# Copies of key and query rows on GpSimd, turned attention blocks in two buffers, block 0 scored earlier: a two-layer decoder trunk

## The chip, the cores and the metric

The kernel runs on one core of a Trainium2 chip. A core has TensorE (matmuls; PE in the profile, PEld its weight loads), VectorE (DVE), ScalarE (ACT), GpSimd (POOL) and SyncE (SP, which here does nothing but issue DMAs), each with a queue of its own that it works off in order. The metric is the device time of one execution in microseconds (us); less is better.

## The reference

Two layers of a decoder trunk over 528 tokens (16 learned meta tokens and 512 of the sequence), 1024 channels. Each layer:

```
h = RMSNorm(x)
[u_pool | z_pool | c_q | c_kv | k_rope | z_mla | g_pool | g_mla] = h @ W_in
y_pool = W_pool_up( PoolMix(u_pool) * silu(z_pool) )
y_mla  = W_mla_up( MLA(c_q, c_kv, k_rope) * silu(z_mla) )
x = x + W_out( sigmoid(g_pool) * y_pool + sigmoid(g_mla) * y_mla )
```

MLA is causal attention of 8 heads. Queries and keys of a head have 64 plain channels and 32 rotary ones, 96 in all, and are normalized over these 96; the rotary part of the key is shared by the heads up to that factor. Values have 64 channels. Everything is float32.

## The kernel before

**Split products.** Each float32 operand is split into a high and a low part, and a product is three matmuls: high by high, high by low, low by high (`mm3`, lines 202, 203, 204). A weight tile comes by DMA into `raw` (line 133, issued by SP), ScalarE makes `whi` (L197), VectorE subtracts and makes `wlo` (L198). `raw`, `whi` and `wlo` have three buffers each.

**Order of the work.** All projections stand in one list (`plan`), which the generator `stream` turns into matmuls bit by bit; each step tells how many nanoseconds of matmuls it put in, and these add up to a clock of the program, `clk`. The attention is written by hand around it: `gap()` and `fill_now()` put matmuls of the list in until the clock has gone on by so much, and `after(ns, fn)` calls `fn` once the clock has gone on by `ns`. `behind(a, b)` makes `a` wait for `b`; `newest` is the last matmul of the list. A scheduler then sets the final order on each engine, so a line's place in the text isn't its place in the queue.

**A head** (`head`, called by `go` for h = 0 to 7 in each layer). The 512 queries are four blocks of 128. Block i sees the 16 meta tokens and the blocks up to itself, so 144, 272, 400 and 528 keys.
- First half: scores of block 1 and of the first `SPL` = 240 keys of block 3 into one PSUM bank (`sa`), of block 2 into another (`sb`). `top` (L824, VectorE) adds the mask, scales, and takes the extreme of each row; `expo` (L831, ScalarE) takes the exponential and the sum of the row. After a `gap`, `turn` moves the 16 meta columns aside (`pm`, L834, GpSimd) and turns blocks 1 and 2 in 32 by 32 pieces (L837, VectorE) into `attD`, a single buffer of 1280 columns.
- Then `pv` of the head before the last (values by probabilities, L950 and L953), and for an odd head the keys of the next pair (`keys`: L779, then the split).
- Second half, after another `gap`: the other 288 keys of block 3, block 0 (three passes, L872) and, in layer 0, the meta queries (L872), in a third bank. Then `top`, `expo`, and `turn` of blocks 3 and 0.
- Out and back: the reciprocal sums go to DRAM (L894), `attD` goes to the DRAM buffer `pdr` in four DMAs (L899) and comes back in one as `attE` (L901), which swaps the 32-row groups; the sums come back spread over 64 partitions (L902). For an odd head `meta_turn` does the like with the meta columns: one store (L916), three loads (L918); GpSimd multiplies the gate by the sums (L906).
- After two more `gap`s: `parts` (L928, L929) splits `attE` for `pv`.

**Keys and queries of a head** (`prep`, called ahead of the head). A head needs one tile with 64 plain and 32 rotary rows for `kh`, `kl`, `qh` and `ql`. The plain rows of the queries are split in place (L791, L794). The other rows come from tiles where they lie on other partitions, by DMAs from SBUF to SBUF that SP issues: 64 rows of the keys for an even head (L797), 32 rotary rows of the keys (L799) and of the queries (L801). That is six DMAs for an even head and four for an odd one. `keys` of the next pair has two buffers, and an even head's tile is the one that the odd head before it has read.

SP issues all of it: weights (L133), the row copies, the stores and loads of the blocks, of the sums and of the meta columns. A DMA that has to wait holds all that stand behind it.

Of the kernel before, what the change touches and what calls it, by code (L numbers as in the profile page):

```python
# [53 lines left out]
RESERVE = ("gm3", "gm3")  # L54
LAG = 2000.0
TAIL = (9000.0, 9000.0)
SPL = 240
RET = 12500.0
WARM = 8
NB = 10  # L60


# [16 lines left out]
def trunk(ctx, tc, xT, xrow, mrow, pos, win, wkr, wqb, wkb, wvb, wgr, wpu, wmu, wout, gains, const, yT):  # L79
# [20 lines left out]
    def tmp(w=W):  # L100
        return tp.tile([P, w], F32, tag="tmp", name=nm("tmp"), bufs=3)

    def att(tag):
        return sl.tile([P, NB * P], F32 if tag == "D" else F32R, tag=f"att{tag}", name=nm(f"att{tag}"), bufs=1 if tag == "D" else 2)

    def wide():
        return tp.tile([P, NB * P], F32R, tag="th", name=nm("th"), bufs=2)
# [1 line left out]
    def halves():  # L109
        for k in range(4, 8):  # L110
            for a, b in FULL:
                yield xb[:, k, a:b]
        for tag in "DE":
            t = att(tag)
            for a in range(4):
                yield t[:, HALF * a:HALF * a + HALF].bitcast(F32)

    def mmt():
# [222 lines left out]
    class Layer:  # L341
# [441 lines left out]
        def prep(self, h):  # L783
            p, odd = h // 2, h % 2
            n0, r0 = (64, 0) if odd else (0, 64)
            kd = self.ks[p][odd]
            g0 = 32 * (h % 4)
            qh, ql = qhl[odd]
            x0 = self.x0
            src = self.qn[p][n0:n0 + 64, x0:T]  # L790
            made = act.activation(qh[n0:n0 + 64, x0:T], src, AF.Copy)  # L791
            if h == 0:
                behind(made, newest[0])
            dve.tensor_sub(ql[n0:n0 + 64, x0:T], src, qh[n0:n0 + 64, x0:T].bitcast(F32))  # L794
            if odd == 0:
                for d, f in zip(kd, self.ks[p][1]):
                    sp.dma_start(d[0:64, :].bitcast(F32), f[0:64, :].bitcast(F32))  # L797
            for d, f in zip(kd, self.kr[h // 4]):
                sp.dma_start(d[r0:r0 + 32, :].bitcast(F32), f[g0:g0 + 32, :].bitcast(F32))  # L799
            for d, f in zip((qh, ql), self.qr[h // 4]):  # L800
                sp.dma_start(d[r0:r0 + 32, x0:T].bitcast(F32), f[g0:g0 + 32, x0:T].bitcast(F32))  # L801
            m = P if odd else QK
            return [t[0:m] for t in (*kd, qh, ql)]

        def head(self, h, kq, prev):
            kh, kl, qh, ql = kq
            odd = h % 2
            nqs = self.nqs
            pa, pb, pc = slot("pa", w=416), slot("cq8"), slot("cq10")
            bia = sm.tile([P, 5], F32, tag="bia", name=nm("bia"), bufs=2)  # L810
            rs = sm.tile([P, 5], F32, tag="rs", name=nm("rs"), bufs=2)
            if odd == 0:
                self.pm = sm.tile([P, 4, 32], F32, tag="pm", name=nm("pm"), bufs=2)
                self.rb = slot("cq11")
            pm, rb = self.pm, self.rb
            blocks = att("D")
            grid = blocks.rearrange("p (b s r) -> p b s r", b=4, s=NB)

            def scores(i, out, a, b):
                q0 = NM + P * i  # L820
                return mm3(out, qh[:, q0:q0 + P], ql[:, q0:q0 + P], kh[:, a:b], kl[:, a:b], True, True)

            def top(i, c, sv, mask):
                return dve.tensor_tensor_reduce(out=sv, in0=sv, in1=mask, scale=nqs[:, i, h:h + 1], scalar=3e38,  # L824
                                                op0=ALU.add, op1=ALU.min, accum_out=bia[:, c:c + 1])

            def causal(n):
                return maskw[:, 512 - n:]

            def expo(i, c, sv, pv):  # L830
                act.activation(pv, sv, AF.Exp, scale=-1.0, bias=bia[:, i:i + 1], accum_out=rs[:, c:c + 1])  # L831

            def turn(i):
                gp.tensor_copy(pm[:, i, 16 * odd:16 * odd + 16], pt[i][:, 0:NM])  # L834
                for j, n in ((0, i + 1),) if i in (0, 1, 3) else ((0, 2), (2, 1)):
                    k = block(i, j)
                    ins = dve.transpose(grid[:, :, k:k + n, :].rearrange("p b s r -> p s b r"), pt[i][:, NM + P * j:NM + P * (j + n)])  # L837
# [9 lines left out]
            top(3, 4, s3, maskw[:, 0:SPL])  # L847
            sb = sct()
            s2 = sb[:, 0:400]
            scores(2, s2, 0, 400)  # L850
            top(2, 2, s2, causal(400))
            expo(1, 1, s1, pt[1])
            expo(2, 2, s2, pt[2])
            if h == 1:
# [12 lines left out]
            sc = sct()  # L867
            s0, s4 = sc[:, 0:144], sc[:, 144:144 + T - SPL]
            scores(3, s4, SPL, T)

            def passes(out, q0, n):
                return [lambda k=k, q=q, x=x: pe.matmul(out, q[:, q0], x[:, 0:n], start=k == 0, stop=k == 2)  # L872
                        for k, (q, x) in enumerate(((qh, kh), (qh, kl), (ql, kh)))]

            todo = passes(s0, slice(NM, NM + P), 144)
            if not self.last:
                sm_ = sc[0:NM, 432:432 + NM]
                todo += passes(sm_, slice(0, NM), NM)
            for fn in todo:
                fn()  # L880
            if not self.last:
                dve.tensor_add(self.smeta[:, h, :], sm_, cst[0:NM, C_MM:C_MM + NM])
            top(3, 3, s4, causal(T - SPL))
            top(0, 0, s0, causal(144))
# [3 lines left out]
            expo(0, 0, s0, pt[0])  # L888
# [4 lines left out]
            row = rdr[self.l][h]  # L893
            sp.dma_start(row.rearrange("a (p i) -> p (a i)", i=4), rs[:, 0:4])  # L894
            got = att("E")
            n = NB * 32
            via = pdr[h % 2]
            for a in range(4):
                sp.dma_start(via[:, n * a:n * a + n].rearrange("(b k) x -> k b x", k=32),  # L899
                             blocks[32 * a:32 * a + 32, :].rearrange("p (b x) -> p b x", x=n))  # L900
            sp.dma_start(got.bitcast(F32), via)  # L901
            sp.dma_start(rb[64 * odd:64 * odd + 64, 0:512], row.partition_broadcast(64))  # L902
            if odd == 1:
                self.meta_turn(pm)
                z = self.zms[h // 2][:, NM:T].rearrange("p (i q) -> p i q", i=4)
                gp.tensor_mul(z, z, rb[:, 0:512].rearrange("p (q i) -> p i q", i=4))  # L906
            return h, got

        def meta_turn(self, pm):
            t = slot("cq9", F32R)  # L910
            f, hi, lo = t[:, 0:P], t[:, P:2 * P], t[:, 2 * P:3 * P]
            dve.transpose(f.bitcast(F32), pm.rearrange("p i r -> p (i r)"))
            split(hi, lo, f.bitcast(F32), 0, P)
            self.mt = slot("racc", F32R)
            via = mdr[0]
            sp.dma_start(via, t[:, P:3 * P].bitcast(F32))  # L916
            for g, c in ((0, 0), (32, 1), (64, 0)):
                sp.dma_start(self.mt[g:g + 32, 0:512].bitcast(F32).rearrange("p (a x) -> p a x", a=4),  # L918
                             via[:, P * c:P * c + P].rearrange("(a r) x -> r a x", a=4))

        def parts(self, prev):
            if prev is None:
                return None
            h, got = prev
            hi, f = wide(), got.bitcast(F32)
            for a in (0, NB * 64):
                b = a + NB * 64
# [336 lines left out]
```

## Time and profile before

| | |
|---|---|
| runs shown | 777.93, 776.76, 777.90 us, median 777.9 |
| profiled execution | 770.3 us, its span 768.5 |
| mean granted TensorE clock | 0.995 |
| TensorE, VectorE, ScalarE, GpSimd busy | 757.2, 537.7, 393.3, 141.1 us |
| attention of layer 0, of layer 1 | about 175 to 310 us, 564 to 690 us |

The profile comes from one execution. Busy shares say how full an engine was. The timeline lists instructions with their start and length; matmuls are pipelined, so their lengths overlap, and what one costs is the distance to the next start. The brackets behind a line tell how long the engine stood idle before it and what released it. The chain of waits follows the work back from the end: at each step what had to come last. "SPq" there is SP issuing a DMA, "DMA a<-b" a transfer under way.

### The profile page before, as it was taken

To read this page: it belongs to the slowest core of one execution; us is meant where nothing else is said; L and a number is where in the kernel's file an instruction comes from. 1 tells how busy PE (TensorE), PEld (TensorE's weight loads), DVE (VectorE), ACT (ScalarE), POOL (GpSimd) and SP (SyncE) were. 2 spreads that over 40 slices of the span, in tenths; PEclk is the share of its full clock that TensorE was granted. 3 is DMA by queue.
4 is the path that set the end of the run, shared out by engine and by line. 5 is a ranking of instruction groups with operands and counts; after the bars stand their busy time and mean duration, and the time that the engine had idled before them with its cause. 6 is when DMAs were issued, how large, how long until landed. Compare 5 with 4: busy or idle time off the path is not lost.

```text
span 768.5 us, 14306 instructions
## 1 busy us (share of the span) xinstructions
PE 757.2 (99%) x5028; PEld 689.0 (90%) x5028; DVE 537.7 (70%) x1211; ACT 393.3 (51%) x864; POOL 141.1 (18%) x187
## 2 busy tenths in 40 slices
PE   9999999999999899999999999999999999999998
PEld 9999999999989899999997898887788788788887
DVE  4588787358889887684366477774578799776832
ACT  5755655545556555543255445455445556554320
POOL 2026404000101010052130264030001110112400
PEclk9999999999999999999999999999999999999999
DMA  7532323336765667425542323234457677673363
GB/s 261 181 109 84 100 80 104 118 124 165 200 201 164 179 201 204 141 83 147 177 143 93 114 83 100 80 89 132 127 158 197 197 207 206 187 214 105 121 196 108
DMA packets 77204, 113.03 MB, mean 147 GB/s; under 512 B 15382, under 2 KB 36246, under 8 KB 77132
## 3 DMA queue, kind: packets, MB, share of 16 engines
q1 hardware_dynamic: 76988, 111.86, 48.4%
q8 instruction: 39, 0.64, 0.3%
q14 instruction: 33, 0.27, 0.1%
q10 hardware_dynamic: 144, 0.26, 0.1%
HBM read 89.76 MB, written 15.86 MB: 137 GB/s over the span
## 4 chain that ended last, share of the span: by engine, by line
PE 85%; DVE 6%; DMA 5%; SPq 1%; issue 1%; ACT 1%; DVEq 0%; ACTq 0%
PE mm L202 26%; PE mm L204 25%; PE mm L203 25%; DMA raw<-win 2%; PE S L202 2%; PE S L204 2%; PE S L203 2%; DVE wlo L198 1%; DVE S L824 1%; DMA kh<-kh 1%; DMA pdr<-attD 1%; PE S L528 1%; PE o L950 1%; PE o L953 1%; DMA mdr<-cq 1%
## 5 line engine op out<-in xcount | busy, mean ns | idle before, releaser
L202 PE MATMUL mm<-hh,whi 128*128 128x264 f32 (+2 forms) x1072 | 338.9, 318 | 5.9 <-ACT whi L197 4.0
L204 PE MATMUL mm<-hh,wlo 128*128 128x264 f32 (+2 forms) x1072 | 338.4, 318 | 0.2 <-DVE wlo L198 0.2
L203 PE MATMUL mm<-hl,whi 128*128 128x264 f32 (+2 forms) x1072 | 337.9, 316 | 0.0
L198 DVE TENSOR_TENSOR wlo<-raw,whi 128x512 fp32r<-128x512 f32 (+2 forms) x242 | 172.5, 715 | 108.5 <-ACT whi L197 103.3
L197 ACT ACTIVATE whi<-raw 128x512 fp32r<-128x512 f32 (+2 forms) x242 | 144.4, 600 | 181.2 <-PE mm L203 126.8
L202 PEld LDWEIGHTS mm<-hh,whi 128*128 128x128 f32 x1072 | 202.7, 189 | 20.2 <-ACT whi L197 4.9
L203 PEld LDWEIGHTS mm<-hl,whi 128*128 128x128 f32 x1072 | 202.8, 189 | 12.4
L204 PEld LDWEIGHTS mm<-hh,wlo 128*128 128x128 f32 x1072 | 202.2, 189 | 12.7 <-DVE wlo L198 0.6
L834 POOL COPY pm<-cq 128x16 f32<-128x16 f32 x32 | 13.3, 416 | 216.5 <-ACT cq L831 216.5
L824 DVE CUSTOM_DVE_ANT_0 S<-S,maskw,nqs 128x240 f32<-128x240 f32 (+4 forms) x80 | 38.3, 499 | 2.3 <-PE S L204 1.7
L642 POOL TENSOR_TENSOR racc<-racc,tmp 128x264 f32<-128x264 f32 (+1 forms) x15 | 14.3, 957 | 134.8 <-ACT tmp L641 134.8
L1025 POOL TENSOR_TENSOR tmp<-tmp,xb 128x264 f32<-128x264 f32 (+1 forms) x24 | 27.1, 1142 | 55.2 <-DVE tmp L1023 53.3
L831 ACT ACTIVATE cq<-S,bia 128x400 f32<-128x400 f32 (+2 forms) x48 | 24.4, 512 | 25.0 <-DVE bia L824 11.9
L202 PE MATMUL mm<-cq,whi 128*128 128x264 f32 (+1 forms) x108 | 34.8, 322 | 0.0
L203 PE MATMUL mm<-th,whi 128*128 128x264 f32 (+1 forms) x108 | 34.7, 321 | 0.0
L202 PE MATMUL mm<-u,whi 128*128 128x264 f32 (+1 forms) x108 | 34.6, 321 | 0.0
L204 PE MATMUL mm<-cq,wlo 128*128 128x264 f32 (+1 forms) x108 | 34.6, 322 | 0.0
L203 PE MATMUL mm<-cq,whi 128*128 128x264 f32 (+1 forms) x108 | 34.6, 321 | 0.0
L204 PE MATMUL mm<-u,wlo 128*128 128x264 f32 (+1 forms) x108 | 34.5, 319 | 0.0
L837 DVE STREAM_TRANSPOSE attD<-cq 128x256 f32<-128x256 f32 (+2 forms) x48 | 21.3, 467 | 12.7 <-DMA pdr<-attD 7.2
L906 POOL TENSOR_TENSOR u<-u,cq 128x512 f32<-128x512 f32 x8 | 12.4, 1552 | 76.4 <-DMA cq<-rdr 26.9
L929 DVE TENSOR_TENSOR attE<-attE,th 128x640 fp32r<-128x640 f32 x32 | 25.1, 809 | 0.5 <-ACT th L928 0.5
(297 smaller groups left out, 1304.7 us busy)
## 6 DMA issues: line engine op xcount, KB each, us to landing
raw<-win SPq DMA_DIRECT2D x143, 256.0 KB, 3.3
pdr<-attD SPq DMA_DIRECT2D x64, 160.0 KB, 3.1
attE<-pdr SPq DMA_DIRECT2D x16, 640.0 KB, 4.9
raw<-wout SPq DMA_DIRECT2D x32, 256.0 KB, 2.9
raw<-wpu SPq DMA_DIRECT2D x16, 256.0 KB, 2.7
raw<-wmu SPq DMA_DIRECT2D x16, 256.0 KB, 2.5
raw<-wqb SPq DMA_DIRECT2D x12, 256.0 KB, 2.6
xb<-xT SPq DMA_DIRECT2D x8, 264.0 KB, 5.6
```

The costliest lines, as they stand in the source:

```text
L197: act.activation(hi[:, :n], raw[:, :n], AF.Copy)
L198: dve.tensor_sub(lo[:, :n], raw[:, :n], hi[:, :n].bitcast(F32))
L202: first = pe.matmul(out, wh, xh, start=start, stop=False)
L203: pe.matmul(out, wh, xl, start=False, stop=False)
L204: newest[0] = pe.matmul(out, wl, xh, start=False, stop=stop)
L642: self.acc_last = gp.tensor_add(self.acc[:, a:b], self.acc[:, a:b], t[:, :b - a])
L824: return dve.tensor_tensor_reduce(out=sv, in0=sv, in1=mask, scale=nqs[:, i, h:h + 1], scalar=3e38, op0=ALU.add, op1=ALU.min, accum_out=bia ...
L831: act.activation(pv, sv, AF.Exp, scale=-1.0, bias=bia[:, i:i + 1], accum_out=rs[:, c:c + 1])
L834: gp.tensor_copy(pm[:, i, 16 * odd:16 * odd + 16], pt[i][:, 0:NM])
L837: ins = dve.transpose(grid[:, :, k:k + n, :].rearrange("p b s r -> p s b r"), pt[i][:, NM + P * j:NM + P * (j + n)])
L929: dve.tensor_sub(got[:, a:b], f[:, a:b], hi[:, a:b].bitcast(F32))
L1025: gp.tensor_add(t[:, :b - a], t[:, :b - a], self.am[m][:, a:b])
```

## The change

1. The row copies of `prep` are GpSimd copies instead of DMAs.
2. Two buffers take the place of `attD`: `attC` with 6 of the 10 pieces (blocks 0, 1, 2) and `attD` with 4 (block 3). Each leaves by one DMA (`away`), `attC` already in the first half. The way back is four DMAs of 32 rows.
3. Block 0 is scored, turned and sent in the first half, in the bank of blocks 1 and 3; `SPL` falls from 240 to 96 to make room.
4. The loads back, the load of the sums, the gate's product and the meta store and loads are put off by `after` (6.5, 6.5, 10.4, 2.6 and 10.4 us of the program's clock) and wait for the newest matmul.
5. One more warm-up matmul (9 instead of 8), and some scratch halves (`halves`) come from the new buffers.

```diff
-SPL = 240
+SPL = 96
+BACK = 6500.0
+LATE = 10400.0
-WARM = 8
+WARM = 9
...
             if odd == 0:
                 for d, f in zip(kd, self.ks[p][1]):
-                    sp.dma_start(d[0:64, :].bitcast(F32), f[0:64, :].bitcast(F32))
+                    gp.tensor_copy(d[0:64, :], f[0:64, :])
             for d, f in zip(kd, self.kr[h // 4]):
-                sp.dma_start(d[r0:r0 + 32, :].bitcast(F32), f[g0:g0 + 32, :].bitcast(F32))
+                gp.tensor_copy(d[r0:r0 + 32, :], f[g0:g0 + 32, :])
             for d, f in zip((qh, ql), self.qr[h // 4]):
-                sp.dma_start(d[r0:r0 + 32, x0:T].bitcast(F32), f[g0:g0 + 32, x0:T].bitcast(F32))
+                gp.tensor_copy(d[r0:r0 + 32, x0:T], f[g0:g0 + 32, x0:T])
...
-            blocks = att("D")
-            grid = blocks.rearrange("p (b s r) -> p b s r", b=4, s=NB)
+            blocks, grid = [], []
+            for tag, n in (("C", 6), ("D", 4)):
+                blocks.append(att(tag, n))
+                grid.append(blocks[-1].rearrange("p (b s r) -> p b s r", b=4, s=n))
+            n, via = NB * 32, pdr[h % 2]
+
+            def away(i):
+                x0, x1 = ((0, 192), (192, n))[i]
+                sp.dma_start(via.rearrange("p (b x) -> p b x", b=4)[:, :, x0:x1], blocks[i].rearrange("p (b x) -> p b x", b=4))
...
-                    if i in (1, 2):
+                    if i != 3:
                         behind(ins, newest[0])
...
-            s1, s3 = sa[:, 0:272], sa[:, 272:272 + SPL]
+            s1, s3, s0 = sa[:, 0:272], sa[:, 272:272 + SPL], sa[:, 368:512]
...
+            for fn in passes(s0, slice(NM, NM + P), 144):
+                fn()
             sb = sct()
...
             turn(1)
             turn(2)
+            turn(0)
+            away(0)
             self.pv(prev)
...
             turn(3)
-            turn(0)
...
-            for a in range(4):
-                sp.dma_start(via[:, n * a:n * a + n].rearrange("(b k) x -> k b x", k=32),
-                             blocks[32 * a:32 * a + 32, :].rearrange("p (b x) -> p b x", x=n))
-            sp.dma_start(got.bitcast(F32), via)
-            sp.dma_start(rb[64 * odd:64 * odd + 64, 0:512], row.partition_broadcast(64))
+            away(1)
...
+            def back():
+                got.append(att("E"))
+                for b in range(4):
+                    behind(sp.dma_start(got[0][32 * b:32 * b + 32, :].bitcast(F32).rearrange("k (a x) -> k a x", a=4),
+                                        via[:, n * b:n * b + n].rearrange("(a k) x -> k a x", a=4)), newest[0])
...
+                behind(sp.dma_start(rb[64 * odd:64 * odd + 64, 0:512], row.partition_broadcast(64)), newest[0])
+
+            def gate():
+                z, rb = self.zms[h // 2][:, NM:T].rearrange("p (i q) -> p i q", i=4), self.rb
+                behind(gp.tensor_mul(z, z, rb[:, 0:512].rearrange("p (q i) -> p i q", i=4)), newest[0])
+
+            after(BACK, back)
+            if odd == 1:
+                after(LATE, gate)
...
+            after(BACK / 2.5, lambda: behind(sp.dma_start(via, t[:, P:3 * P].bitcast(F32)), newest[0]))
+            after(LATE, back)
```

In the last two lines, `back` is the function of `meta_turn` that holds the three loads of the meta columns. `parts` now steps the list until the loads back of its head have been put in.

More of the change, by code (lines that the diff above doesn't have):

```diff
@@ L112, in halves @@
                 yield xb[:, k, a:b]
-        for tag in "DE":
-            t = att(tag)
-            for a in range(4):
+        for tag, n in (("C", 6), ("D", 4), ("E", NB), ("E", NB)):
+            t = att(tag, n)
+            for a in range(n * P // HALF):
                 yield t[:, HALF * a:HALF * a + HALF].bitcast(F32)
@@ L835, in turn @@
                 for j, n in ((0, i + 1),) if i in (0, 1, 3) else ((0, 2), (2, 1)):
-                    k = block(i, j)
-                    ins = dve.transpose(grid[:, :, k:k + n, :].rearrange("p b s r -> p s b r"), pt[i][:, NM + P * j:NM + P * (j + n)])
-                    if i in (1, 2):
+                    g, k = grid[i // 3], block(i, j) - 6 * (i // 3)
+                    ins = dve.transpose(g[:, :, k:k + n, :].rearrange("p b s r -> p s b r"), pt[i][:, NM + P * j:NM + P * (j + n)])
+                    if i != 3:
                         behind(ins, newest[0])
@@ L847, in head, with passes @@
             top(3, 4, s3, maskw[:, 0:SPL])
+            def passes(out, q0, n):
+                return [lambda k=k, q=q, x=x: pe.matmul(out, q[:, q0], x[:, 0:n], start=k == 0, stop=k == 2)
+                        for k, (q, x) in enumerate(((qh, kh), (qh, kl), (ql, kh)))]
+            for fn in passes(s0, slice(NM, NM + P), 144):
+                fn()
             sb = sct()
@@ L867, in head @@
             sc = sct()
-            s0, s4 = sc[:, 0:144], sc[:, 144:144 + T - SPL]
+            s4 = sc[:, 0:T - SPL]
             scores(3, s4, SPL, T)
[L871 to L875, printed above, removed]
             if not self.last:
                 sm_ = sc[0:NM, 432:432 + NM]
[L878 to L881, printed above, removed]
+                for fn in passes(sm_, slice(0, NM), NM):
+                    fn()
                 dve.tensor_add(self.smeta[:, h, :], sm_, cst[0:NM, C_MM:C_MM + NM])
             top(3, 3, s4, causal(T - SPL))
-            top(0, 0, s0, causal(144))
             dve.tensor_tensor(out=bia[:, 3:4], in0=bia[:, 3:4], in1=bia[:, 4:5], op=ALU.min)
@@ L913, in meta_turn, with back @@
             split(hi, lo, f.bitcast(F32), 0, P)
-            self.mt = slot("racc", F32R)
             via = mdr[0]
[L916 to L919, printed above, removed]
+            def back():
+                self.mt = slot("racc", F32R)
+                for g, c in ((0, 0), (32, 1), (64, 0)):
+                    ins = sp.dma_start(self.mt[g:g + 32, 0:512].bitcast(F32).rearrange("p (a x) -> p a x", a=4),
+                                       via[:, P * c:P * c + P].rearrange("(a r) x -> r a x", a=4))
+                    behind(ins, newest[0])
+            after(BACK / 2.5, lambda: behind(sp.dma_start(via, t[:, P:3 * P].bitcast(F32)), newest[0]))
+            after(LATE, back)
         def parts(self, prev):
@@ L924, in parts @@
             h, got = prev
+            while not got:
+                step()
+            got = got[0]
             hi, f = wide(), got.bitcast(F32)
```

20 lines of the change are left out of this document (9 added, 11 removed).

## The prediction

> **What bounds the kernel now.** I read the page's busy shares first, then the stretches that hold the two attention phases, then what TensorE waited for.
>
> ```profile
> PE 757.2 (99%) x5028; PEld 689.0 (90%) x5028; DVE 537.7 (70%) x1211; ACT 393.3 (51%) x864; POOL 141.1 (18%) x187
> ```
> ```profile
> 190.00:320.00 130.00, 126.77 (x1000) 124.18 (x999) 106.46 (x287) 73.40 (x184) 13.12 (x32) 0.99 0.64 187
> 565.00:700.00 135.00, 131.94 (x633) 109.62 (x632) 110.96 (x268) 75.87 (x178) 17.36 (x36) 0.99 0.68 193
> 220.00:250.00 30.00, 30.00 (x242) 29.54 (x242) 28.57 (x78) 18.94 (x48) 3.93 (x9) 1.00 0.63 184
> 600.00:650.00 50.00, 49.43 (x236) 41.53 (x237) 47.44 (x114) 32.50 (x78) 7.17 (x15) 0.97 0.68 195
> 260.00:270.00 10.00, 8.12 (x50) 7.93 (x51) 9.32 (x25) 6.62 (x17) 0.39 (x2) 0.83 0.55 160
> 600.00:610.00 10.00, 9.43 (x39) 7.99 (x40) 9.02 (x23) 7.74 (x20) 1.90 (x4) 0.83 0.55 139
> ```
>
> (Columns: length, then PE, PEld, DVE, ACT, POOL busy, granted clock, DMA share, GB/s.) TensorE is busy 757.2 of 768.5 us, and the change leaves its number of matmuls alone. So a gain can come only from the holes in TensorE's stream. VectorE stands behind it at 82% in both attention phases (106.46 of 130, 110.96 of 135) and at 95% in 220 to 250 and 600 to 650. GpSimd is nearly empty, 13.1 and 17.4 us.
>
> The holes, in the timeline of PE (start, length, line, form, idle before it and its releaser):
>
> ```profile
> 176.18 0.28 PE L204 MATMUL mm<-hh,wlo 128*128 128x264 f32 x1
> 176.84 0.55 PE L202 MATMUL S<-kh,qhl 96*128 96x272 f32 x2 [0.38 <-DMA kh<-kh]
> ```
> ```profile
> 212.96 0.28 PE L203 MATMUL mm<-hl,whi 128*128 128x264 f32 x1
> 213.08 0.28 PE L204 MATMUL mm<-hh,wlo 128*128 128x264 f32 x1
> 214.32 0.39 PE L202 MATMUL mm<-hh,whi 128*128 128x264 f32 x1 [0.96 <-ACT whi L197]
> 214.55 0.28 PE L203 MATMUL mm<-hl,whi 128*128 128x264 f32 x1
> 215.04 0.39 PE L204 MATMUL mm<-hh,wlo 128*128 128x264 f32 x1 [0.21 <-DVE wlo L198]
> ```
> ```profile
> 259.43 0.40 PE L965 MATMUL mm<-racc,vb 96*128 96x512 f32 x1
> 261.66 0.39 PE L202 MATMUL mm<-hh,whi 128*128 128x264 f32 x1 [1.83 <-DVE tmp L655]
> ```
> ```profile
> 266.83 0.28 PE L204 MATMUL mm<-hh,wlo 128*128 128x264 f32 x1
> 267.34 0.36 PE L202 MATMUL S<-kh,qhl 96*128 96x272 f32 x1 [0.23 <-DMA kh<-kh]
> ```
> ```profile
> 598.39 0.29 PE L203 MATMUL S<-kl,qhl 128*128 128x272 f32 x1
> 600.57 0.50 PE L202 MATMUL mm<-hh,whi 128*128 128x512 f32 x1 [1.89 <-ACT whi L197]
> ```
> ```profile
> 659.52 0.39 PE L203 MATMUL mm<-hl,whi 128*128 128x512 f32 x1
> 659.76 0.40 PE L204 MATMUL mm<-hh,wlo 128*128 128x512 f32 x1
> 661.33 0.50 PE L202 MATMUL mm<-hh,whi 128*128 128x512 f32 x1 [1.17 <-ACT whi L197]
> ```
>
> Matmuls overlap, so I count from start to start: 0.12 us after 264 or 272 columns (212.96 to 213.08), 0.24 after 512 (659.52 to 659.76). What is over is lost: 0.54 at 176, 1.12 and 0.37 at 213, 2.0 at 259, 0.39 at 267, 2.06 at 598, 1.33 at 660. Behind the two gaps of 2 us the clock falls: the slices 260:270 and 600:610 have 0.83, which is 0.17 x 10 = 1.7 us lost each. The sum is 7.8 + 3.4 = 11.2 us, the most that attention has to give.
>
> The chain of waits (start, length, what) says where the weights were late:
>
> ```profile
> 205.71 2.68 DMA mdr<-cq
> 208.45 0.49 SPq L918
> 208.98 0.46 SPq L918
> 209.96 3.60 DMA raw<-win
> ```
> ```profile
> 591.49 2.65 DMA mdr<-cq
> ...
> 596.30 3.50 DMA raw<-win
> ```
> ```profile
> 655.76 0.04 SPq L916
> 655.85 4.78 DMA raw<-win
> ```
>
> At 213 and 598 SP's queue stood 2.7 us behind the landing of the meta store (L916) that the L918 loads wait for, and the weight load behind them started that much late. At 660 it is the same queue: the weight load goes out right after SP was let past L916, whose data VectorE had only just turned. At 176 and 267 the row copies themselves were late. Only the hole at 259 has VectorE as its last releaser (L655, emptying a bank).
>
> **The change part by part.**
>
> *Row copies off SP.* Forty copies a layer (6 for an even head, 4 for an odd) become GpSimd copies of 528 columns, and their issues leave SP: 80. The stores of turned blocks go from 64 issues to 32, their loads from 16 to 64. SP so has 64 issues fewer, near 0.5 us each (the L918 rows). GpSimd's price, by the groups of 60 to 300 us (busy, mean ns of one, idle before):
>
> ```profile
> L834 POOL COPY pm<-pa 128x16 f32<-128x16 f32 x16 | 3.1, 196 | 6.1 <-ACT pa L831 5.6 <-DMA kl<-kl 0.5
> L508 POOL COPY kp<-kp 32x264 f32<-32x264 f32 x6 | 3.0, 506 | 3.2 <-DVE kp L506 3.0
> ```
>
> From 196 ns for 16 columns to 506 for 264 is 1.25 ns a column, so 528 columns take 0.84 us, waits included. A layer has 40 x 0.84 = 34 us more on an engine that was busy 13 of 130: room. The even heads are the tight ones, since the copies write a buffer that the odd head before has just read: 6 x 0.84 + 0.2 for a copy of L834 ahead = 5.2 us. In the built order 70 matmuls of 264 columns (8.5 us) stand between the last score of head 1 and the first of head 2 in layer 0, and 12 us of them in layer 1. So no hole; one opens when a copy takes over 1.4 us. The two holes on `kh` (0.54 + 0.39) go.
>
> *What the copies do to VectorE.* The line that feeds the six L508 copies of layer 0, by its source (shortest, median, longest in ns):
>
> ```profile
> L506 DVE TENSOR_TENSOR kp<-kp,rinv x2: 421/524/627, 60.1 to 60.7; 128x264 f32<-128x264 f32 x2
> ```
>
> The same product of two SBUF tiles took 421 ns ahead of the copies (60.1) and 627 among them (60.7): 0.2 us lost. A copy can cost VectorE nothing (it waits itself) or its whole length, 0.84. I take 0.2, the row that shows it: 8 us a layer. [...]
>
> *Two buffers and one store each.* Transposes that waited for the single buffer's stores:
>
> ```profile
> DVE attD L837 <- DMA pdr<-attD: 8.4, 4, 3.0
> ```
> ```profile
> pdr<-attD SPq DMA_DIRECT2D x64, 160.0 KB, 3.1
> ```
>
> The first is the answer for 190 to 320; such waits go, because the first buffer leaves half a head earlier. Against 8 us lost to copies this is even in layer 0. In layer 1 VectorE is the poorer by most of its 8 us and has 24 us to spare. So I leave the VectorE hole at 259 (2.0 + 1.7 us) standing; bounds 0 and twice that. The stores now have 768 and 512 bytes in a piece in place of 1280. Their landing is not in the trace; the old one takes 3.1 us (second row, issue to landing), so I bound it by half and twice that. The loads stand 6.5 us of matmuls later, so even twice hides.
>
> *Loads and meta rows put off.* The L918 loads now stand 7.8 us of matmuls behind their store, instead of right behind it. Then SP doesn't stand 2.7 us, and the weight loads at 213, 598 and 660 start in time: 1.12 + 0.37 + 2.06 + 1.33 gone, and with 598 its 1.7 us of half clock. What is late next is VectorE's half of the weights (L198).
>
> *Block 0 in the first half.* What VectorE does there, one after the other for two blocks:
>
> ```profile
> L824 DVE CUSTOM_DVE_ANT_0 S<-S,maskw,nqs 128x240 f32<-128x240 f32 (+4 forms) x80 | 38.3, 499 | 2.3 <-PE S L204 1.7
> ```
>
> The same three passes now wait for two of these (1.0 us), because they share a bank with their scores. The built order puts them 3.8 to 8 us of matmuls behind those scores. Covered unless VectorE lags over 2.8 us; then such a head pays the rest. Block 3 is divided into 96 and 432 columns instead of 240 and 288, 528 in both. By columns that is free; if a pass of 96 costs as much as one of 264 (0.12 instead of 0.04), it is 0.24 us a head, 3.8 for sixteen. I take 0.04 a head, 0.6, near the lower end, since the weights of a pass are loaded beside the pass before.
>
> *The ninth warm-up product.*
>
> ```profile
> 1.05 3.78 PE L155 MATMUL wps<-ones 128*128 128x128 f32 x16 [1.05 <-DVE na L754]
> 5.18 0.99 PE L202 MATMUL S<-hh,th 128*128 128x264 f32 x2 [0.35 <-ACT hh L364]
> ```
>
> An eighth of 3.78 is 0.47, so the idle 0.35 fills and the first score starts 0.12 late. Closing that hole might lift the clock a step of 3.4 us (the two slices at 0.83) earlier, worth 1.7. Bounds -1.7 and +0.12; I take 0.
>
> **The sum**, against the profiled execution (770.3 us, span 768.5): row copies -0.93, weight holes -4.88, half clock -1.7, split +0.6, together -6.9, so 763.4. The median of the runs shown is 777.9; I carry the difference of 7.6 over and forecast 777.9 - 6.9 = **771.0 us**. [...]
>
> **The rivals.**
>
> 1. *VectorE's hole goes too.* For it: 8.4 us of its waits go in that phase. A further -3.7, and -1.7 if the warm-up step counts: 767.3 to 765.6. Against it: the copies.
> 2. *The wait moves* (the change doesn't do what it says). SP still waits: a store for its transposes, a load for its matmul, with weights behind them. In the built order up to ten issues stand between two weight loads; ten at 0.5 us plus one landing of 3 is 8 us, against three weight tiles ahead of 12 matmuls or 2.8 us each. For it: 8 of 8.4 leaves no slack there. Against it: the longest of its waits (L918) is put off. The 4.88 + 1.7 come back: 778.
> 3. *VectorE becomes the bound* (slower). Each copy blocks it for its whole length. A phase of 130 us has 40, so 220:250 has nine, which add 7.6 to 28.57 of 30, 6 over; 600:650 has fifteen, 12.6 on 47.44 of 50, 10 over. That is +16 - 6.9 = +9 with nothing hidden (787), and +1 (779) if the weights, three tiles ahead, hide 4 in each stretch; I take 783. With a loss of x a copy the two stretches go 24x - 4 over, so it decides from x = 0.45 us. Against it: the 0.2 of the one row.
>
> **How the numbers follow.** Forecast (768 to 774 by itself) 0.43; rival 1 0.25; rival 2 0.07; rival 3 0.25. A measurement of this kernel tells about 0.2% from no change. Faster 0.68, same 0.06, slower 0.26. The low end takes rival 1 with as much again from the 7.6 us that the profile doesn't show, should these be stalls of the same kind: 762. The high end is rival 3 with most of it unhidden, 785; about 0.1 is left out above and as much below.
>
> **What would show it.** Right: no TensorE hole over 1 us released by ACT `whi` with `raw` behind it in the chain; SP not waiting at the meta loads; granted clock 1.00 in 600:610; the wait of `attD` for its store gone; copies at 0.6 to 0.9 us. Wrong: VectorE over 95% through both phases with L198 or L929 well over 0.7 and 0.8 us; first scores of a head released by POOL; block 0's passes released by VectorE; or a new hole behind SP's stores.

## The result and the profile after

The changed kernel takes 787.1 us (785.5 to 787.9), the kernel before 777.6 (776.8 to 777.9): 9.5 us more, ratio 1.0148, interval 1.0100 to 1.0195. The forecast was 771.0, with 785 as the high end. By the profiled executions (span 768.5 and 785.9) the loss is 17.4 us, because the profiled execution of before is 7.6 us faster than the median of its runs; what follows accounts for these 17.4. The times of the kernel before vary between chips and from run to run on one chip, 765.7 to 779.7 in the experiments below, so every ratio there is with runs of the same chip.

The page of the changed kernel, busy times:

```profile
PE 763.6 (97%) x5030; PEld 689.3 (88%) x5030; DVE 551.1 (70%) x1211; ACT 395.5 (50%) x864; POOL 209.5 (27%) x267
```

GpSimd has 68 us more, as reckoned (2 x 34), VectorE 13. The stretches of the two attention phases, the two crowded stretches, and two in which the clock fell (columns as in the prediction):

```profile
190.00:320.00 130.00, 128.78 (x1017) 125.29 (x1016) 114.55 (x294) 76.12 (x189) 36.98 (x60) 1.00 0.66 174
565.00:700.00 135.00, 121.82 (x564) 98.45 (x563) 106.43 (x253) 69.07 (x166) 39.77 (x65) 0.97 0.55 148
220.00:250.00 30.00, 30.00 (x237) 29.09 (x237) 29.79 (x77) 18.42 (x47) 11.54 (x19) 1.00 0.69 181
600.00:650.00 50.00, 40.86 (x182) 32.19 (x181) 42.09 (x102) 26.76 (x64) 18.57 (x25) 0.93 0.48 127
```
```profile
642.00:652.00 10.00, 8.71 (x29) 6.89 (x30) 9.94 (x25) 6.00 (x18) 2.45 (x6) 0.66 0.37 112
707.00:717.00 10.00, 9.20 (x32) 7.21 (x31) 6.84 (x11) 5.17 (x9) 0.05 (x1) 0.66 0.43 130
```

Layer 0 gained: TensorE 128.8 of 130 at a clock of 1.00, where it had 126.8 at 0.99. With the projections' matmuls counted off one by one, the changed kernel is 4.0 us ahead at the end of layer 0 and still at the 3500th (556 us), ahead of the attention of layer 1; at the 4000th (725 us), behind it, it is 17.4 behind. All of the loss, 21.4 us, lies in the attention of layer 1. VectorE isn't full there: 42.1 of 50 between 600 and 650, less than the 47.4 before. TensorE waits, and each of the two stretches with a clock of 0.66 (10 us long, 0.34 short of full) costs 3.4 us more.

What TensorE waited for from 165 to 720 us (total, times, longest; the four longest rows, 13.5 of 17.2 us), and what the engines ahead of it waited for:

```profile
PE o L976 <- ACT th L954: 6.7, 4, 3.2
PE o L979 <- DVE attE L955: 2.9, 3, 1.1
PE S L976 <- ACT th L954: 2.0, 1, 2.0
PE o L976 <- DVE tmp L985: 1.9, 1, 1.9
```
```profile
ACT th L954 <- DMA attE<-pdr: 34.1, 9, 6.4
DVE attE L955 <- ACT th L954: 30.0, 9, 6.4
```

(L954 and L955 are `parts`, L928 and L929 before; L976 and L979 are `pv`, which for the last head writes a bank named `S`.) Before, L928 never waited for `attE`, and L929 had 0.5 us of idle time ahead of it. The groups of both kernels (busy, mean ns, idle before):

```profile
L929 DVE TENSOR_TENSOR attE<-attE,th 128x640 fp32r<-128x640 f32 x32 | 25.1, 809 | 0.5 <-ACT th L928 0.5
```
```profile
L955 DVE TENSOR_TENSOR attE<-attE,th 128x640 fp32r<-128x640 f32 x32 | 31.8, 1025 | 30.0 <-ACT th L954 30.0
```

The return of a head is the way of its turned blocks to DRAM and back as `attE`. Now it comes late, ScalarE stands 34 us and VectorE 30 with all that is queued behind them, and TensorE stands at the products with the values. SP's timeline of one such return (stores L825, loads L911), then the last step of it in the chain of waits and TensorE's timeline:

```profile
613.61 0.52 SPq L825 DMA_DIRECT2D pdr<-attC  x1
614.23 0.58 SPq L825 DMA_DIRECT2D pdr<-attD  x1
614.86 0.72 SPq L135 DMA_DIRECT2D raw<-win  x1
617.79 0.33 SPq L911 DMA_DIRECT2D attE<-pdr  x1
618.22 0.38 SPq L904 DMA_DIRECT2D rdr<-rs  x1
618.64 1.38 SPq L911 DMA_DIRECT2D attE<-pdr  x3
```
```profile
619.60 4.57 DMA attE<-pdr
```
```profile
624.08 0.40 PE L205 MATMUL mm<-hl,whi 128*128 128x512 f32 x1
625.69 0.51 PE L976 MATMUL o<-th,vt 128*128 128x512 f32 x1 [1.21 <-ACT th L954]
```

The loads go out 3.6 us behind the second store, about when it lands (3.5 us by the page of the profile), the last lands at 624.2, ScalarE begins the split at 624.27, and the product starts 1.4 us behind that: nothing in this chain is slack. And the first buffer leaves 0.6 us ahead of the second here, not half a head.

### The profile page after: what moved, and what is told of

Same layout as the page of the kernel before. It is cut to its first block, busy times and chain, and to the rows that moved or that the text cites. A ratio compares the mean times of both kernels' runs of the same rounds, so it can differ in the third digit from the quotient of the medians.

```text
span 785.9 us, 14368 instructions
## 1 busy us (share of the span) xinstructions
PE 763.6 (97%) x5030; PEld 689.3 (88%) x5030; DVE 551.1 (70%) x1211; ACT 395.5 (50%) x864; POOL 209.5 (27%) x267
## 4 chain that ended last, share of the span: by engine, by line
PE 77%; DVE 9%; DMA 8%; issue 2%; ACT 2%; SPq 2%; ACTq 0%; DVEq 0%
PE mm L204 23%; PE mm L206 23%; PE mm L205 23%; DMA attE<-pdr 4%; DMA pdr<-attD 2%; DVE attE L955 2%; PE S L205 1%; PE S L206 1%; DVE S L832 1%; PE S L204 1%; DVE wlo L200 1%; SPq L911 1%; DMA raw<-win 1%; ACT th L954 1%; PE S L530 1%
## 5 line engine op out<-in xcount | busy, mean ns | idle before, releaser
L200 DVE TENSOR_TENSOR wlo<-raw,whi 128x512 fp32r<-128x512 f32 (+2 forms) x242 | 176.5, 732 | 94.8 <-ACT whi L199 91.4
L206 PEld LDWEIGHTS mm<-hh,wlo 128*128 128x128 f32 x1072 | 201.9, 189 | 12.7 <-DVE wlo L200 0.3
L955 DVE TENSOR_TENSOR attE<-attE,th 128x640 fp32r<-128x640 f32 x32 | 31.8, 1025 | 30.0 <-ACT th L954 30.0
L644 POOL TENSOR_TENSOR racc<-racc,tmp 128x264 f32<-128x264 f32 (+1 forms) x15 | 14.4, 960 | 134.4 <-ACT tmp L643 134.4
L954 ACT ACTIVATE th<-attE 128x640 fp32r<-128x640 f32 x32 | 21.8, 731 | 38.9 <-DMA attE<-pdr 34.1
L832 DVE CUSTOM_DVE_ANT_0 S<-S,maskw,nqs 128x144 f32<-128x144 f32 (+4 forms) x80 | 37.7, 494 | 2.7 <-PE S L206 1.7
L839 ACT ACTIVATE cq<-S,bia 128x400 f32<-128x400 f32 (+2 forms) x48 | 24.5, 514 | 21.4 <-DVE bia L832 13.5
L842 POOL COPY pm<-cq 128x16 f32<-128x16 f32 x32 | 12.1, 377 | 77.8 <-ACT cq L839 77.3
L801 POOL CAST kh<-cq 32x528 fp32r<-32x528 f32 x16 | 13.7, 858 | 70.3 <-issue 36.5
```

The costliest lines, as they stand in the source:

```text
L200: dve.tensor_sub(lo[:, :n], raw[:, :n], hi[:, :n].bitcast(F32))
L206: newest[0] = pe.matmul(out, wl, xh, start=False, stop=stop)
L644: self.acc_last = gp.tensor_add(self.acc[:, a:b], self.acc[:, a:b], t[:, :b - a])
L801: gp.tensor_copy(d[r0:r0 + 32, :], f[g0:g0 + 32, :])
L954: behind(act.activation(hi[:, a:b], f[:, a:b], AF.Copy), newest[0])
L955: dve.tensor_sub(got[:, a:b], f[:, a:b], hi[:, a:b].bitcast(F32))
```

## The experiments

The **built order** is the order in which the scheduler has put the instructions, which can be read before a run. Two measures of it, in us of projections (0.46 ns a column, by the 0.12 us of 264 columns and the 0.24 of 512 in the timeline of before): the distance of a head's first scores from those of the head before, and that of its first product with the values from its own first scores. For layer 1 (counted in the traces, the figures come out the same within 2 us):

| kernel | scores to scores | scores to products |
|---|---|---|
| before | 6.3 13.6 7.9 14.9 9.0 14.9 9.5 | 20 26 24 29 26 29 24 27 |
| changed | 9.6 17.7 6.2 17.7 6.3 18.5 5.3 | 25 22 23 24 23 21 19 22 |
| rows by DMA (e3) | 6.1 13.9 8.3 14.4 10.4 13.5 10.4 | 20 26 24 28 26 27 26 26 |
| pinned (e5) | 11.3 11.9 11.3 12.7 11.3 12.7 11.3 | 23 26 23 27 23 27 27 26 |
| with products (e10) | 5.6 11.3 11.9 12.1 11.9 12.1 11.9 | 20 26 27 27 27 27 27 26 |

I first took the put-off return for the cause (theory A). Theories A, B and C are told in the text ahead of e1, D (the order) and E (the copies come too late) in the one ahead of e5.

**e1, the return put off less.**

```diff
-            after(BACK, back)
+            after(2600.0, back)
```

(The run has the 2600 in a constant of its own.)

> Changed kernel, with the loads of the turned blocks (L911) and of the row factors (L916) put off by 2600 instead of 6500 ns of matmuls. Theory A (the put-off loads land after the turn of their readers in layer 1, and ScalarE and VectorE, which work in order, stand behind them): the 33.6 us that L954 waits for attE, and the TensorE holes ahead of L976, go; 766 to 773 us. Theory B (GpSimd's row copies take VectorE's time, the third rival of the prediction): nothing changes, 784 to 788. Theory C (the gate product L920 runs beside the subtraction L955 and makes it 2 us long): the gate waits for the factors, so it moves off too; 766 to 773.

785.8 us, ratio 1.0134 (1.0089 to 1.0180). Theory A is out. Why, say ScalarE's wait from 565 to 710 us (34.1 in the changed kernel) and SP's timeline (lines stand one further down than in the changed kernel):

```profile
ACT th L955 <- DMA attE<-pdr: 27.4, 7, 7.0
```
```profile
616.98 0.58 SPq L826 DMA_DIRECT2D pdr<-attD  x1
617.61 0.72 SPq L136 DMA_DIRECT2D raw<-win  x1
620.54 0.33 SPq L912 DMA_DIRECT2D attE<-pdr  x1
```

The load goes out 3.6 us behind its store, as in the changed kernel: it waits for the store, and the store for the turning. For this return the program's clock had no part in it.

**e2, the gate's product put off more.**

```diff
-                after(LATE, gate)
+                after(15000.0, gate)
```

> Changed kernel, with only the gate product (L920) put off by 15000 instead of 10400 ns of matmuls, past the parts of the same head. Theory A: 783 to 788, the waits of L954 for attE stay near 34 us. Theory B: 784 to 788. Theory C: L955 falls back from 1025 to about 815 ns and the time to 768 to 775.

785.0, ratio 1.0143 (1.0105 to 1.0181). The experiment missed its aim: the subtraction's mean stayed at 1064 ns (median 819, longest 2173), with a gate product at 641.62 us for 1.53, and whether the two still met isn't shown. What it leaves open, e3 and e10 answer below.

**e4, only the four `attE` loads put off less,** the row factors (the last DMA of `back`) not.

```diff
-            after(BACK, back)
+            after(2600.0, back)
+            after(BACK, factors)
```

(Not shown: `factors` is the last part of `back`, now a function of its own.)

> Changed kernel, with only the four attE loads put off by 2600 instead of 6500 ns; the row factors stay at 6500, so the gate stays about where it is. Theory A: 767 to 775, the waits of L954 for attE go. Theory B: 784 to 788. Theory C: 783 to 788, and L955 stays near 1025 ns.

786.6, ratio 1.0157 (1.0122 to 1.0192); ScalarE waits 34.1 us for `attE`. Against A once more; B and C both allow it.

**e3, the row copies back on SP as DMAs,** the rest of the change kept.

```diff
-                gp.tensor_copy(d[r0:r0 + 32, :], f[g0:g0 + 32, :])
+                sp.dma_start(d[r0:r0 + 32, :].bitcast(F32), f[g0:g0 + 32, :].bitcast(F32))
```

(and the other two lines of `prep` alike)

> Changed kernel, with only the row copies put back on SP as DMAs, as in the kernel before. Theory A: 784 to 792, since the loads stay late and SP gets 80 issues more. Theory B: 768 to 774. Theory C: 784 to 790.

763.9, ratio 0.9868 (0.9831 to 0.9905). So with the GpSimd copies the kernel is 22 us slower than without, and all the rest together makes it 1.3% faster. A and C are out, since both said 784 or more here. The page and ScalarE's wait for the return, which was 34.1:

```profile
PE 755.6 (99%) x5030; PEld 687.1 (90%) x5030; DVE 542.5 (71%) x1211; ACT 396.5 (52%) x864; POOL 149.4 (20%) x187
```
```profile
ACT th L954 <- DMA attE<-pdr: 0.6, 1, 0.6
```

Theory B had the direction (768 to 774), but in two ways it doesn't fit: VectorE is busy 542.5 us here and 551.1 in the changed kernel, 8.6 apart, not 22; and in the changed kernel it stands idle for 30. The table above shows what else the copies change: the order. In the changed kernel the heads of layer 1 come in pairs, the second 5 to 6 us behind the first (9.6 in the first pair), the next pair 18 us later, and from the second head on a head has 19 to 24 us up to its products where e3 has 24 to 28. The kernel's context asks the scheduler to set the order by a simulated timeline (its last lines), so an operation that changes engine can move others. That the order costs the time is theory D.

**e7, one part alone: kernel before with the rows on GpSimd** (e3's edit the other way round, in the kernel before).

> Kernel before with one part of the change alone: the row copies on GpSimd. Built order: scores 6.2 to 15.8 us of projections apart in layer 1, 19 to 26 us from scores to products (before: 6.3 to 14.9 and 20 to 29). Theory D: slower than before by 3 to 12 us, with ScalarE or VectorE waiting for attE in layer 1. Theory B: slower by 10 to 25 us with VectorE over 95 per cent busy. The prediction's forecast for this part: 0.9 us faster.

776.3 against 771.7, ratio 1.0072 (1.0046 to 1.0098). Within D's range and below B's; the forecast of this part (0.9 us faster) was wrong by itself, and with the rest of the change its price grows from 0.7 to 2.8% (1.0148 / 0.9868). As D had said, ScalarE now waits for `attE`, which the kernel before never did; here that costs little. This wait and two holes of the profile:

```profile
ACT th L928 <- DMA attE<-pdr: 29.7, 10, 5.2
```

```profile
224.98 0.29 PE L202 MATMUL mm<-hh,whi 128*128 128x264 f32 x1
228.23 0.39 PE L202 MATMUL mm<-hh,whi 128*128 128x264 f32 x1 [2.97 <-DVE tmp L655]
...
666.89 0.40 PE L202 MATMUL mm<-hh,whi 128*128 128x512 f32 x1
669.53 0.79 PE L950 MATMUL o<-th,vt 128*128 128x512 f32 x1 [2.24 <-ACT th L928]
```

**e5, the changed kernel with TensorE's order held,** by dependencies that only the scheduler sees, from the first head of a layer to the last (not shown: `pinned` is set ahead of a layer's heads and cleared behind them):

```diff
     def mm3(out, wh, wl, xh, xl, start, stop):
         first = pe.matmul(out, wh, xh, start=start, stop=False)
+        if pinned[0]:
+            follow(first, newest[0])
```

> Changed kernel, row copies on GpSimd as they are; only the matmuls of the projections and of the scores are held in the order of the program during the heads (each group of three follows the one before), so that a head's scores stand 11 to 13 us of projections behind those of the head before (built order) instead of 5.3 to 18.5. Theory D (the scheduler, which works out its order from the durations that it expects, sets the heads in uneven pairs once the rows are GpSimd copies; the second head of a pair then has 19 to 24 us of projections between its scores and its products with the values instead of 26 to 28, and its return is late): 763 to 770, ScalarE's waits for attE under 5 us. Theory B (the copies take VectorE's time): 783 to 788. Theory E (the copies themselves are done too late): 775 or more, with TensorE holes ahead of first scores released by GpSimd.

791.5, ratio 1.0278 (1.0236 to 1.0319): D's time is missed by over 20 us, and 791 lies in what E had said and some 3 us above B. One of D's signs came out all the same: ScalarE waits only 0.5 us for `attE`. TensorE's waits:

```profile
PE o L982 <- DVE attE L958: 9.5, 5, 2.8
PE S L204 <- POOL kh L802: 5.7, 2, 4.2
```

5.7 us stand at the first heads of the two layers, whose scores can't move any more while their rows are made. 9.5 stand at the products, which I hadn't held: for the first three even heads of layer 1 (three of the five waits) the scheduler put them 23 us behind the scores, 3 to 4 us less than where the rows come by DMA (e6). The return is in time there, but VectorE's subtraction is not: ahead of the wait at 631 us VectorE works without a gap and comes to it 0.9 us after ScalarE is done. Theory E fits these rows, but not the changed kernel: there no wait of TensorE is released by GpSimd.

**e6, its control with the rows by DMA** (e5's edit on e3).

> The same holding of the order, with the rows copied by DMA on SP (control for e5). Theory D: within 4 us of the rows by DMA without it (763.9), whose heads stood 8 to 14 us apart already. Theory B: the same, and 18 us or more under e5. Theory E: the same, and 8 us or more under e5.

776.1, ratio 1.0070 (1.0042 to 1.0098). D had said within 4 us of 763.9, so it missed too: the first heads again.

```profile
PE S L204 <- DMA kh<-kh: 6.5, 2, 5.0
```

No product waits over 0.5 us here; they stand 26 to 27 us behind the scores in layer 1. e5 and e6 differ by 15 us, and what e5 has among TensorE's waits and e6 hasn't is the products (and behind such waits a lower clock, 0.985 against 0.993 in the mean).

**e8, e5 with each row copy made twice.**

```diff
                 gp.tensor_copy(d[r0:r0 + 32, :], f[g0:g0 + 32, :])
+                gp.tensor_copy(d[r0:r0 + 32, :], f[g0:g0 + 32, :])
```

> e5 with every row copy made twice, one behind the other: 80 more GpSimd copies of 0.85 us. Theory D: 0 to 5 us over e5. Theory B: 15 to 25 us over e5, as the first 80 copies would have cost. Theory E: 5 to 15 us over e5, at the first scores of even heads.

(and the other two lines of `prep` alike)

815.6, ratio 1.0585 (1.0545 to 1.0626): 24 us over e5, as B said; D had said 0 to 5. By itself this looked like the price of a copy. But the mean granted clock fell from 0.985 to 0.966, which by the two spans is 28 us of lost clock against 12 (814.2 x 0.034 and 789.7 x 0.015): by this estimate some 16 of the 24 us are the clock behind TensorE's holes, not VectorE's time.

```profile
PE o L985 <- DVE attE L961: 12.3, 6, 3.1
PE S L204 <- POOL kh L803: 10.3, 2, 6.1
```

**e9, the price of the copies with nothing waiting for them:** e3 plus 80 GpSimd copies of the same shapes from the same sources into an idle buffer (shown is one of three such loops).

```diff
+            for f in self.kr[h // 4]:
+                behind(gp.tensor_copy(idle[0:32], f[g0:g0 + 32, :]), newest[0])
```

> Rows by DMA (e3), plus the 80 GpSimd copies of the same shapes from the same sources into a buffer that nobody reads: what they do to VectorE is there, nothing waits for them, and the built order of the other engines stays (16 of 4929 TensorE and 36 of 1201 VectorE instructions stand elsewhere). Theory B (VectorE's time, taken by the copies, is the 22 us between e3 and the changed kernel): 776 to 786. Theory D (the order is): 764 to 768; VectorE's busy time 6 to 12 us over e3.

763.4, ratio 0.9854 (0.9822 to 0.9887), no different from e3 (0.9868). The copies ran and VectorE paid:

```profile
PE 752.9 (99%) x5030; PEld 685.1 (90%) x5030; DVE 550.9 (72%) x1211; ACT 395.4 (52%) x864; POOL 209.8 (28%) x267
```

550.9 less 542.5 is 8.4 us for 80 copies, 0.1 us each, and the time doesn't show it. Theory B falls as the cause.

**e10, e5 with the products held too,** and the holding begun behind the first head:

```diff
-            hosts, last = list(hosts), [None]
+            hosts, last = list(hosts), [newest[0] if pinned[0] else None]
...
                 now = self.head(h, kq, late)
+                pinned[0] = True
```

> Changed kernel, row copies on GpSimd; projections, scores and now the products with the values too are held in the order of the program from the second head of a layer on (built order: scores 11 to 12 us of projections apart, products 26 to 28 us behind their scores, as with the rows by DMA). Theory D, with the products as what was left out in e5: 764 to 772, and no holes ahead of the products of even heads. Theory B: 780 to 790, with VectorE's queue late.

766.5, ratio 0.9900 (0.9864 to 0.9936), with the very copies on GpSimd that the changed kernel has. Layer 1 and its wait for the return:

```profile
565.00:700.00 135.00, 131.65 (x625) 108.13 (x624) 117.26 (x258) 75.37 (x174) 41.43 (x65) 1.00 0.65 174
```
```profile
ACT th L957 <- DMA attE<-pdr: 3.4, 4, 1.6
```

34 us of waiting have become 3.4, and VectorE does more in the same stretch than in the changed kernel (117.3 against 106.4). The gate product still meets the subtraction here (GpSimd, then VectorE), so that isn't what cost the time either:

```profile
627.44 1.56 POOL L923 TENSOR_TENSOR u<-u,cq 128x512 f32<-128x512 f32 x1 [3.42 <-DMA pdr<-attC]
```
```profile
627.62 2.80 DVE L958 TENSOR_TENSOR attE<-attE,th 128x640 fp32r<-128x640 f32 x2 [0.99 <-ACT th L957]
```

**e11, the same holding with the rows by DMA** (e10's edit on e3).

> Control for e10: the same holding with the rows by DMA. Both theories: 763 to 770 (e3 763.9, and the 10 us that e5 and e6 lost at the first head of each layer are not held here). Theory D: within 4 us of e10. Theory B: 12 us or more under e10.

767.0, ratio 0.9897 (0.9866 to 0.9928). With TensorE's order held alike, copies on GpSimd and DMAs on SP give the same time. And the holding by itself is no gain: with the rows by DMA it is 0.9897 with it and 0.9868 without.

**e12, e3 with the meta store and loads at once again.**

```diff
-            after(BACK / 2.5, lambda: behind(sp.dma_start(via, t[:, P:3 * P].bitcast(F32)), newest[0]))
-            after(LATE, back)
+            sp.dma_start(via, t[:, P:3 * P].bitcast(F32))
+            back()
```

> Rows by DMA (e3), with the store and the loads of the meta rows issued at once behind one another, as in the kernel before, instead of put off. By the prediction's step for the weights, SP stands at the loads again and the holes at weights come back: 4.9 us, and 1.7 us of half clock behind a hole of 2 us, over e3 (0.987 of before): 0.994 to 0.998 of before. If the weights' holes went for another reason (SP has fewer issues), within 2 us of e3, 0.985 to 0.989.

(The loads then don't wait for the newest matmul any more.) 768.5, ratio 0.9917 (0.9891 to 0.9943): between the two forecasts, 0.5% over e3, with intervals that overlap. SP stands at the meta loads again (L937, waiting for their store: nothing goes out from 619.35 to 622.16 us), where in e3 those of 590.64 follow 0.1 us behind the DMA ahead, and yet no hole has weights behind it: the step of the prediction isn't borne out. Where its holes are:

```profile
614.24 0.36 PE L204 MATMUL S<-kh,qhl 96*128 96x272 f32 x1 [1.19 <-DMA kh<-cq]
```
```profile
633.38 0.45 PE L975 MATMUL o<-attE,vt 128*64 128x512 f32 x1 [1.47 <-DVE attE L951]
```
```profile
647.59 0.55 PE L204 MATMUL S<-kh,qhl 96*128 96x272 f32 x2 [1.63 <-DMA kh<-kh]
```

**What they say together.** The changed kernel is slow by the order that came with the copies: with the copies left as they are and TensorE's order held, it is 1.0% faster than before, 2.4% under the changed kernel (0.9900 / 1.0148). What is argued, not shown: that the scheduler sets pairs because it expects the copies to be done sooner or later than DMAs. And not tried: the uneven order with rows by DMA. So whether the order alone costs the 22 us, or the order with the 8 us that VectorE loses in it, stays open; e8 (24 us in a tight order) and e9 (nothing in a loose one) speak for both having a part, as does e5, where VectorE was late at products that stood too near.

## Why the prediction was wrong

- **What bounds the kernel:** right. TensorE's stream and its holes decide, all the way through.
- **The step that failed** is in the row copies: "In the built order 70 matmuls of 264 columns (8.5 us) stand between the last score of head 1 and the first of head 2 in layer 0, and 12 us of them in layer 1. So no hole". The copies were priced as work in a given order, at -0.93 us for the holes that they close; by e3 they cost 22 us with the order that came with them. I read the built order for one pair of heads and for the copies' own slack, and took the rest of the order as it was. The copies were in time (no wait of TensorE is released by GpSimd), and yet moved the scores and the products of the other heads against the projections. What the runs show in place of "no hole" is 34.1 us of ScalarE waiting for returns and 13.5 us of TensorE waiting at the products; with the same copies and the order held (e10) the first is 3.4 and the time 2.4% less. Why the scheduler set this order stays open. In the table this could be read beforehand: 18.5 and 5.3 us where 14.9 and 9.5 had been, 19 where 24 had been.
- "The loads stand 6.5 us of matmuls later, so even twice hides" was wrong in the same place. Nothing was worked out against the products that read the load. In layer 1 these stand 19 to 25 us behind the scores, and the chain of turning, store, load and split left no slack there.
- **The copies' lengths:** 0.84 us forecast, 837 to 920 ns measured for 32 rows (691 to 720 for 64):

```profile
L803 POOL CAST qhl<-q 32x528 fp32r<-32x528 f32 (+1 forms) x32 | 28.9, 920 | 9.1 <-PE S L858 7.7 <-ACT q L298 0.5
L801 POOL CAST kl<-cq 32x528 fp32r<-32x528 f32 x16 | 13.4, 837 | 2.2 <-PE S L858 1.1 <-POOL pm L842 0.7
```

- **What they do to VectorE:** 0.2 us a copy taken, 0.1 measured in e9. The direction was right and the size half. One meeting cost more: in the pair of rows from e10 the gate product began at 627.44, the subtraction at 627.62, and its two halves took 2.80 us, where two take 1.6 by the 809 ns of the kernel before. The mean over all copies is far below a copy's whole length (0.84), the loss that rival 3 took.
- **Rival 3** gave 779 to 787 and the time fell there (787.1), but that is luck, for its mechanism is not what happened: VectorE is at 79% in layer 1 (106.4 of 135) and waits. In 220 to 250 it is nearly full (29.79 of 30, as the rival feared) and TensorE stood there for none of it (30.00 of 30).
- **Two buffers:** forecast was that the first leaves half a head earlier. In SP's timeline the two stores of a head stand 4.3 to 7.6 us apart for four heads of layer 0, but 0.6 to 2.0 for the other four and 0.6 to 1.1 for seven of eight in layer 1.
- **The weights' holes** (-4.88, and 1.7 of half clock) did go, in the changed kernel and in e3. The reason given, the put-off meta loads, isn't borne out: in the changed kernel SP still stands at them for 10.7 us in six waits (17.1 in six before), in e3 it doesn't at those of 590.64, in e12 it does again (2.8 us at 622.16), and the weights' holes are gone in all three. What else brought the weights in time wasn't separated. SP's waits at the loads of `attE` grew from 9.2 to 21.2 us in the changed kernel.
- **The rest of the change** (all but the row copies) was put at -6.0 us, and e3 measures -1.3%, some 10 us by the medians; by the profiled executions (764.4 against 768.5) it is 4.1.
- **Row holes** (-0.93): gone in the changed kernel. With the rows by DMA a longer one comes up in e3, which the copies would close:

```profile
610.70 0.40 PE L206 MATMUL mm<-hh,wlo 128*128 128x512 f32 x1
614.62 0.54 PE L204 MATMUL S<-kh,qhl 96*128 96x272 f32 x2 [3.52 <-DMA kh<-cq]
```

- **The VectorE hole at 259** was left standing. It is gone in the changed kernel, in e3 and in e10; rival 1 was right on that. The changed kernel has another of 1.1 us at 265, ahead of a product.
- **The ninth warm-up product:** 0, with -1.7 as a bound. The changed kernel is 1.2 us ahead after the first 100 matmuls of projections, since the full pace comes earlier than in the profile of before (0.12 us from start to start from 5.82 us on, in before only from 10.59). But it comes earlier in e7 too, which has eight products and a longer hole ahead of the first score (0.59 us against 0.35 before); here the same stretch of before and of e7:

```profile
7.29 0.42 PE L204 MATMUL S<-hh,th 128*128 128x264 f32 x1
7.51 0.42 PE L203 MATMUL mm<-hl,th 128*128 128x264 f32 x1
```
```profile
7.33 0.28 PE L202 MATMUL S<-hh,th 128*128 128x264 f32 x1
7.45 0.41 PE L202 MATMUL mm<-hh,th 128*128 128x264 f32 x2
```

It is 0.22 us from start to start before and 0.12 in e7, so the ninth product isn't needed for the earlier moment; whether it helps isn't shown.

- **The signs of being right** came for the most part (no hole behind weights, copies near 0.84 us, a clock of 1.00 from 600 to 612), while the time went the other way: they were set where the old holes had been. Of the signs of being wrong, the new hole behind SP's stores is the one that came.
- **The 7.6 us** between the profile of before and its median were carried over. The changed kernel doesn't have them (787.9 profiled, 787.1 median), nor e3 (766.3 and 763.9). They belong to that profile of the kernel before, and stay unexplained.

## What to carry to other kernels

Where a scheduler sets the order, a change of engine for one operation is a change of the order of all: before a time is forecast, the built order of both kernels is compared for every repetition, producers to readers, not at one place. A return trip that engines stand waiting for (ScalarE 34.1 us here, VectorE 30.0 behind it) holds up what is queued there, so its slack belongs in the sum. And a price found by doubling (e8) holds for that order only; the same copies with nobody waiting (e9) cost nothing that the runs could tell (0.9854 against 0.9868).

The faster kernels here keep the rest of the change: rows by DMA (0.9868), or rows on GpSimd with TensorE's order held (0.9900).

## What the hardware showed beside that

- The length of a gap alone didn't tell what it cost in clock. Before, gaps of 2.0 (259) and 2.06 us (598) were each followed by 0.83 over 10 us (0.50 in 263.2 to 266.5 and in 601.2 to 604.5). In the changed kernel those of 3.4 (638) and 2.2 us (704) were followed by 0.66 over 10 (0.50 in 642.9 to 649.6 and in 707.7 to 714.5), while behind those of 2.0 (600) and 1.9 us (672) the clock stayed at 1.00:

```profile
672.00:682.00 10.00, 6.57 (x34) 5.07 (x34) 8.24 (x20) 5.22 (x11) 1.72 (x2) 1.00 0.31 103
600.00:612.00 12.00, 9.18 (x46) 7.03 (x45) 11.91 (x31) 7.71 (x20) 5.06 (x4) 1.00 0.31 94
```

- 80 GpSimd copies that nobody waits for took 8.4 us of VectorE's time (e9 against e3), 0.1 us each in the mean. A VectorE subtraction that began 0.18 us behind a GpSimd product (e10) took 2.80 us for two halves, against 1.6 by the 809 ns of the kernel before.
